# Gate matmuls whose f16 one-hot operands step by 4 bytes in place of 8

## The chip, the cores and the metric

The kernel runs on one core of a Trainium2 chip. What counts is the device time of one execution in microseconds (us); the number given is the median of three runs. The engines are TensorE (PE, with its weight loads PEld), VectorE (DVE), ScalarE (ACT), GpSimd (POOL) and SyncE (SP).

## What is computed

Two transformer blocks on 256 tokens of width 1,024. Each ends in a product-key retrieval ("peer"), which is where the change lies: for each token 8 heads pick 16 experts each out of 128 x 128, and the block adds a weighted sum over the picked experts.

```python
e = i1 * N_KEYS + i2                      # 8 heads x 16 picks per token
g = jax.nn.softmax(c_top, axis=-1)
ue = jnp.take(u, e, axis=0)
ve = jnp.take(v, e, axis=0)
act = gelu(einsum('thkd,td->thk', ue, xb))
return einsum('thk,thkd->td', g * act, ve)
```

## The kernel before

No row of `u` or `v` is gathered. The kernel multiplies all tokens with all experts, 128 experts of one `i2`-row at a time, and lets a gate be zero where a token did not pick an expert. The work of `Peer.run`, once in each of the two blocks:

- 16 tiles of the query projection, and on DVE the two rounds of top 16 (`retrieve`), whose result is, for each token, 128 pairs of indices (`self.ij`, f16) and 128 weights, held as two f16 numbers whose sum is the weight (`self.w`). The 128 picks of a token lie on the 128 partitions.
- 128 steps over `e`. Each is a tile of `u` times all tokens, `k.tile_ch()`: 24 matmuls (L187) of 256 columns, since every f32 operand is split into a high and a low part (`hi`, `lo`; `hi` is copied by ACT at L152, `lo` is subtracted by DVE at L157, two tiles ahead, three buffers each). Then `gelu` writes the activations into `a0` or `a1`. The tiles of `u` and `v` come by DMA, 512 KB each.
- 128 steps over the rows of `v`: 12 matmuls each (L261) of 512 columns.

The gates run in the background of the second part, by a generator (`gates`) that is advanced by a budget of DVE time after each tile (`k.step(BUD[0])`). For 8 tokens at a time DVE makes three f16 tiles of 1,024 elements in a partition: `o1`, the one-hot of the first index (L511), `ow[0]`, the one-hot of the second (L513), and twice its product with a weight part (L516, for `ow[1]` and then `ow[0]`). Per token two matmuls (L525) with `o1` as weights and `ow[0]`, `ow[1]` as moving operand add up the 128 x 128 gates of that token in PSUM; 4 tokens (`TB`) fill a bank, and 8 matmuls. DVE multiplies a bank into the activations that are there already (L531), ACT copies the gates of experts that are not yet computed (L533). The matmuls of a chunk are issued one chunk after its one-hots (`pend`). The tiles of one-hots have two buffers each.

A tile of one-hots lies as `[P, NB, P, TB]`: for each of `NB` = 2 groups of 4 tokens, 128 key values, and innermost the 4 tokens. The DVE instructions then run over 4 neighbouring elements, and a matmul, which wants the 128 key values of one token, reads every fourth element: a step of 4 f16, 8 bytes.

The order of instructions on each engine comes from a scheduler that simulates a timeline when the kernel is built; each engine runs its own list in order.

Of the kernel before, what the change touches and what calls it, by code (L numbers as in the profile page):

```python
# [11 lines left out]
F16 = mybir.dt.float16  # L12
# [7 lines left out]
P = 128  # L20
T = 256
# [386 lines left out]
BUD = [1.6, 1.6]  # L408
CUT = [0, 1024, 640]
TB = 4  # L410
NB = 2
LAST = 2
EARLY = 1
HB = 4
# [15 lines left out]
class Peer:  # L430
# [72 lines left out]
    def gates(self):  # L503

        k, nc = self.k, self.k.nc
        pend = deque()
        for t0 in range(0, T, NB * TB):
            o1, *ow = [self.oh.tile([P, NB, P, TB], F16, name=n, tag=n, bufs=2) for n in ("o1", "ow0", "ow1")]
            some = lambda a: a[:, t0:t0 + NB * TB].rearrange("p (b t) -> p b t", b=NB).unsqueeze(2).to_broadcast([P, NB, P, TB])
            iota = self.iota.unsqueeze(1).to_broadcast([P, NB, P, TB])  # L510
            nc.vector.tensor_tensor(out=o1, in0=iota, in1=some(self.ij[:, 0]), op=ALU.is_equal)  # L511
            yield 0.64
            nc.vector.tensor_tensor(out=ow[0], in0=iota, in1=some(self.ij[:, 1]), op=ALU.is_equal)  # L513
            yield 0.64
            for q in (1, 0):
                nc.vector.tensor_tensor(out=ow[q], in0=ow[0], in1=some(self.w[:, q]), op=ALU.mult)  # L516
                yield 0.64
            for n in range(NB):
                pend.append((t0 + n * TB, o1[:, n], [o[:, n] for o in ow]))
            while len(pend) > NB or (pend and t0 + NB * TB >= T):  # L520
                t1, o1, ow = pend.popleft()
                tag, g = k.bank([P, TB, P])
                for n in range(TB):
                    for q in range(2):
                        nc.tensor.matmul(out=g[:, n, :], lhsT=o1[:, :, n], rhs=ow[q][:, :, n], start=(q == 0), stop=(q == 1))  # L525
                yield 0.0
                ts = slice(t1, t1 + TB)
                gi = g.rearrange("p t i -> p i t")
                for a, lo, hi, e in self.slots(0, self.acted):
                    v = a[:, lo:hi, ts]  # L530
                    nc.vector.tensor_tensor(out=v, in0=gi[:, e:e + hi - lo], in1=v, op=ALU.mult)  # L531
                for a, lo, hi, e in self.slots(self.acted, P):
                    nc.scalar.activation(out=a[:, lo:hi, ts], in_=gi[:, e:e + hi - lo], func=ACTF.Copy)  # L533
                self.gated = t1 + TB
                k.done(tag)
                yield 0.00105 * TB * self.acted + 0.12
# [13 lines left out]
    def run(self, after):  # L550

        k, nc = self.k, self.k.nc
        b = self.b
        with ExitStack() as es:
            pool = lambda name: es.enter_context(k.tc.tile_pool(name=f"{name}{b}", bufs=1))
            self.oh = pool("oh")
            idx = pool("idx")
            self.iota = idx.tile([P, P, TB], F16, name="iota")
            self.k16 = k.const(idx, "iota16")
            self.ij = idx.tile([P, 2, T], F16, name="ij")  # L560
            self.w = idx.tile([P, 2, T], F16, name="w")
# [3 lines left out]
            tks = k.tc.tile_pool(name=f"tk{b}", bufs=1)  # L565
            tk = tks.__enter__()
            self.a0 = ap0.tile([P, SPLIT, T], F32, name="a0")
            nc.vector.tensor_copy(out=self.iota, in_=k.const(tk, "iota").unsqueeze(2).to_broadcast([P, P, TB]))
            skT = tk.tile([P, 16, P], F32, name="skT")
            nc.scalar.dma_start(out=skT, in_=k.i[f"sk{b}"])  # L570
            st = tk.tile([P, 2, 16, 16], F32, name="st")
# [67 lines left out]
            for n in range(P - LAST):  # L639
# [9 lines left out]
                a, w = parts.popleft(), k.weights()  # L649
# [984 lines left out]
```

## Time and profile before

| | |
|---|---|
| median of 3 runs (lowest, highest) | 2301.98 us (2300.34, 2302.52) |
| the profiled execution | 2302.45 us, of which the span of instructions is 2300.7 |
| granted TensorE clock, mean | 0.992 |
| busy, share of the span | PE 97%, PEld 90%, DVE 67%, ACT 51%, POOL 36% |
| moved by DMA | 370.90 MB, mean 161 GB/s |

Busy time of an engine is the union of its instructions' times. On PE matmuls overlap: a record lasts from a start to a modelled end, and the next one starts earlier than that. PEld are weight loads, which overlap with matmuls. Some few records can be missing from a trace. Durations are those of one profiled execution.

### The profile page before, as it was taken

The page shows a single profiled execution, that of the slowest core. Times are in us where ns is not written, and L with a number is a line of the kernel's source. Part 1 is how long each engine was busy: PE and PEld are TensorE (multiplying, and loading weights), DVE is VectorE, ACT ScalarE, POOL GpSimd, SP SyncE. Part 2 cuts the span into 40 slices and gives each one's busy share as a digit, 9 for nine tenths or more (in the row PEclk, how much of TensorE's full clock was granted, in tenths as well). Part 3 has the DMA queues.
Part 4 walks back from the last instruction along what each step waited for, and adds up shares of the span by engine and source line. Part 5 has one row for each costly group of instructions (what it writes and reads, how often), then busy time and mean ns, then how long its engine had stood idle before and what let it go on. Part 6 is the DMA issues. An engine that isn't in the chain of part 4 may idle for free. (4 is left out here: it accounts for less than half of the span.)

```text
span 2300.7 us, 41435 instructions
## 1 busy us (share of the span) xinstructions
PE 2234.7 (97%) x15512; PEld 2077.6 (90%) x15512; DVE 1543.4 (67%) x3119; ACT 1167.0 (51%) x2210; POOL 833.7 (36%) x626
## 2 busy tenths in 40 slices
PE   8999999999999999988899999999999999999998
PEld 8989999999988888878899898999999999888887
DVE  4669976788644544479756787699677885444444
ACT  5644544444455555565444555445444444555554
POOL 3453000000066666645553775620000000666665
PEclk9999999999999999999999999999999999999999
DMA  5455554444556666633334244556544445666664
GB/s 186 151 176 171 183 162 155 141 144 139 166 191 204 199 194 195 193 108 117 123 110 129 74 130 143 171 166 188 168 147 139 138 146 170 195 202 194 193 193 155
DMA packets 103881, 370.90 MB, mean 161 GB/s; under 512 B 12928, under 2 KB 14080, under 8 KB 103424
## 3 DMA queue, kind: packets, MB, share of 16 engines
q1 hardware_dynamic: 101808, 365.21, 50.6%
q10 hardware_dynamic: 1872, 3.04, 0.4%
q8 instruction: 122, 2.00, 0.3%
q14 instruction: 79, 0.65, 0.1%
HBM read 367.16 MB, written 1.05 MB: 160 GB/s over the span
## 5 line engine op out<-in xcount | busy, mean ns | idle before, releaser
L157 POOL TENSOR_TENSOR lo<-raw,hi 128x384 fp32r<-128x384 f32 (+2 forms) x428 | 706.9, 1654 | 1387.3 <-ACT hi L152 1348.2
L152 ACT ACTIVATE hi<-raw 128x1024 fp32r<-128x1024 f32 x684 | 724.3, 1060 | 741.9 <-PE mm L187 458.6
L187 PE MATMUL mm<-xh,hi 128*128 128x256 f32 x3168 | 919.6, 290 | 17.3 <-ACT cvx L1007 7.1
L187 PE MATMUL mm<-xh,lo 128*128 128x256 f32 x3168 | 902.5, 285 | 0.4 <-DVE lo L157 0.4
L187 PE MATMUL mm<-xl,hi 128*128 128x256 f32 x3168 | 897.4, 283 | 1.2 <-DVE xl L309 1.0
L157 DVE TENSOR_TENSOR lo<-raw,hi 128x640 fp32r<-128x640 f32 (+2 forms) x654 | 664.0, 1016 | 340.5 <-ACT hi L152 337.8
L187 PEld LDWEIGHTS mm<-xh,hi 128*128 128x128 f32 x3168 | 604.5, 191 | 22.2 <-ACT cvx L1007 8.7
L187 PEld LDWEIGHTS mm<-xl,hi 128*128 128x128 f32 x3168 | 605.4, 191 | 2.3 <-DVE xl L309 1.6
L187 PEld LDWEIGHTS mm<-xh,lo 128*128 128x128 f32 x3168 | 599.0, 189 | 0.6 <-DVE lo L157 0.6
L261 PE MATMUL y<-lo,ah 128*128 128x512 f32 x1024 | 398.4, 389 | 0.1
L261 PE MATMUL y<-hi,ah 128*128 128x512 f32 x1024 | 397.4, 389 | 0.0
L261 PE MATMUL y<-hi,al 128*128 128x512 f32 x1024 | 275.9, 389 | 0.0
L615 DVE TENSOR_TENSOR al<-a,ah 128x256 fp32r<-128x256 f32 x256 | 118.5, 464 | 191.4 <-PE y L261 191.0
L261 PEld LDWEIGHTS y<-lo,ah 128*128 128x128 f32 x1024 | 192.1, 188 | 40.7 <-POOL lo L157 0.6
L261 PEld LDWEIGHTS y<-hi,ah 128*128 128x128 f32 x1024 | 192.3, 188 | 39.9
L261 PEld LDWEIGHTS y<-hi,al 128*128 128x128 f32 x1024 | 192.2, 188 | 39.9
L614 ACT ACTIVATE ah<-a 128x256 fp32r<-128x256 f32 x256 | 106.5, 417 | 167.6 <-PE y L261 165.9
L525 PEld LDWEIGHTS <-o 128*128 128x128 f16 x1024 | 105.1, 118 | 6.9
L525 PE MATMUL by<-ow,o 128*128 128x128 f16 x672 | 94.8, 296 | 0.0
L516 DVE TENSOR_TENSOR ow<-ow,w 128x1024 f16<-128x1024 f16 x128 | 87.4, 685 | 0.1
L513 DVE TENSOR_TENSOR ow<-iota,ij 128x1024 f16<-128x1024 f16 x64 | 44.3, 692 | 54.5 <-PE by L525 38.6
L543 ACT ACTIVATE a<-mm 128x256 f32<-128x256 f32 (+33 forms) x228 | 69.0, 303 | 0.0
(500 smaller groups left out, 2006.7 us busy)
## 6 DMA issues: line engine op xcount, KB each, us to landing
raw<-in_u_dram SPq DMA_DIRECT2D x256, 512.0 KB, 3.5
raw<-in_v_dram SPq DMA_DIRECT2D x256, 512.0 KB, 4.3
raw<-in_w_in_dram SPq DMA_DIRECT2D x108, 512.0 KB, 3.5
raw<-in_wq_dram SPq DMA_DIRECT2D x32, 512.0 KB, 3.5
raw<-in_w_out_dram SPq DMA_DIRECT2D x16, 512.0 KB, 3.5
raw<-in_w_branch_a_dram SPq DMA_DIRECT2D x8, 512.0 KB, 3.5
raw<-in_w_branch_b_dram SPq DMA_DIRECT2D x8, 512.0 KB, 3.5
skT<-in_sk_dram ACTq DMA_DIRECT2D x2, 1024.0 KB, 5.2
```

The source lines that it names most:

```text
L152: self.nc.scalar.activation(out=h, in_=r, func=ACTF.Copy)
L157: eng.tensor_tensor(out=l[:, a:b], in0=r[:, a:b], in1=h[:, a:b].bitcast(F32), op=ALU.subtract)
L187: self.nc.tensor.matmul(out=ps, lhsT=a[:, c, :], rhs=b, start=(c == 0 and k == 0), stop=(c == NC - 1 and k == 2))
L261: i = self.nc.tensor.matmul(out=self.y[tt][dh], lhsT=p[:, ts], rhs=q[:, ds], start=(first and m == 0), stop=(last and m == 2))
L513: nc.vector.tensor_tensor(out=ow[0], in0=iota, in1=some(self.ij[:, 1]), op=ALU.is_equal)
L516: nc.vector.tensor_tensor(out=ow[q], in0=ow[0], in1=some(self.w[:, q]), op=ALU.mult)
L525: nc.tensor.matmul(out=g[:, n, :], lhsT=o1[:, :, n], rhs=ow[q][:, :, n], start=(q == 0), stop=(q == 1))
L543: nc.scalar.activation(out=a[:, s, n:T], in_=ps[:, n:T], func=ACTF.Gelu)
L614: nc.scalar.activation(out=h, in_=a, func=ACTF.Copy)
L615: nc.vector.tensor_tensor(out=l, in0=a, in1=h.bitcast(F32), op=ALU.subtract)
```

## The change

The tiles of one-hots lie with `OT` = 2 tokens innermost, `[P, 4, P, 2]` in place of `[P, 2, P, 4]`. A bank still holds 4 tokens, which now come from two groups. The operands of a gate matmul step by 2 f16, 4 bytes. The tiles keep their size, DVE's instructions their number and their 1,024 elements; `self.iota`, the table that the indices are compared with, has 256 elements in a partition in place of 512, and so has its copy. Built, the two kernels have the same instructions in the same order on every engine, but for that copy.

```diff
-NB = 2
+OT = 2
+NB = 8 // OT
...
-        for t0 in range(0, T, NB * TB):
-            o1, *ow = [self.oh.tile([P, NB, P, TB], F16, name=n, tag=n, bufs=2) for n in ("o1", "ow0", "ow1")]
-            some = lambda a: a[:, t0:t0 + NB * TB].rearrange("p (b t) -> p b t", b=NB).unsqueeze(2).to_broadcast([P, NB, P, TB])
-            iota = self.iota.unsqueeze(1).to_broadcast([P, NB, P, TB])
+        for t0 in range(0, T, NB * OT):
+            o1, *ow = [self.oh.tile([P, NB, P, OT], F16, name=n, tag=n, bufs=2) for n in ("o1", "ow0", "ow1")]
+            some = lambda a: a[:, t0:t0 + NB * OT].rearrange("p (b t) -> p b t", b=NB).unsqueeze(2).to_broadcast([P, NB, P, OT])
+            iota = self.iota.unsqueeze(1).to_broadcast([P, NB, P, OT])
...
-            for n in range(NB):
-                pend.append((t0 + n * TB, o1[:, n], [o[:, n] for o in ow]))
-            while len(pend) > NB or (pend and t0 + NB * TB >= T):
-                t1, o1, ow = pend.popleft()
+            one = lambda a, t: a[:, t // OT, :, t % OT]
+            for t1 in range(0, NB * OT, TB):
+                pend.append((t0 + t1, [[one(a, t1 + n) for a in (o1, *ow)] for n in range(TB)]))
+            while len(pend) > NB * OT // TB or (pend and t0 + NB * OT >= T):
+                t1, hot = pend.popleft()
...
-                        nc.tensor.matmul(out=g[:, n, :], lhsT=o1[:, :, n], rhs=ow[q][:, :, n], start=(q == 0), stop=(q == 1))
+                        nc.tensor.matmul(out=g[:, n, :], lhsT=hot[n][0], rhs=hot[n][1 + q], start=(q == 0), stop=(q == 1))
...
-            self.iota = idx.tile([P, P, TB], F16, name="iota")
+            self.iota = idx.tile([P, P, OT], F16, name="iota")
...
-            nc.vector.tensor_copy(out=self.iota, in_=k.const(tk, "iota").unsqueeze(2).to_broadcast([P, P, TB]))
+            nc.vector.tensor_copy(out=self.iota, in_=k.const(tk, "iota").unsqueeze(2).to_broadcast([P, P, OT]))
```

## Rows read from the trace of the kernel before

**Rows 1.** The page's head: busy us and share; granted clock in 40 slices.

```profile
PE 2234.7 (97%) x15512; PEld 2077.6 (90%) x15512; DVE 1543.4 (67%) x3119; ACT 1167.0 (51%) x2210; POOL 833.7 (36%) x626
...
PEclk9999999999999999999999999999999999999999
```

**Rows 2.** Instructions of L525: duration ns min/median/max, first and last start.

```profile
L525 PEld LDWEIGHTS <-o x1024: 111/117/141, 303.1 to 1904.6; 128*128 128x128 f16 x171
L525 PE MATMUL by<-ow,o x672: 277/297/304, 308.2 to 1904.7; 128*128 128x128 f16 x168
```

**Rows 3.** Stretches: length, busy PE, PEld, DVE, ACT, POOL, clock, DMA.

```profile
400.00:600.00 200.00, 200.00 (x1675) 197.54 (x1673) 157.82 (x294) 85.89 (x214) 0.00 (x0) 1.00 0.46 143
...
1800.00:1850.00 50.00, 50.00 (x421) 49.38 (x420) 40.95 (x76) 20.39 (x51) 0.00 (x0) 1.00 0.45 142
```

**Rows 4.** Waits: 400 to 600 us; those for L525, whole kernel; PE's own.

```profile
ACT hi L152 <- PE mm L187: 104.5, 54, 3.4
...
  DVE ow L513: 54.5, 58
...
PE mm L187 <- DVE lo L157: 0.4, 1, 0.4
```

**Rows 5.** Timeline of PE and PEld around gate matmuls: start us, length us.

```profile
507.30 2.05 PE L525 MATMUL bg<-ow,o 128*128 128x128 f16 x16
...
514.70 0.28 PE L187 MATMUL mm<-xl,hi 128*128 128x256 f32 x1
514.82 0.28 PE L187 MATMUL mm<-xh,lo 128*128 128x256 f32 x1
514.93 1.11 PE L525 MATMUL by<-ow,o 128*128 128x128 f16 x8
...
514.93 0.34 PEld L525 LDWEIGHTS <-o 128*128 128x128 f16 x4
...
515.75 0.21 PEld L187 LDWEIGHTS mm<-xh,hi 128*128 128x128 f32 x1
```

**Rows 6.** Timeline of PE in the second matmul stage.

```profile
900.54 0.39 PE L261 MATMUL y<-lo,ah 128*128 128x512 f32 x1
900.77 1.07 PE L261 MATMUL y<-hi,al 128*128 128x512 f32 x4
```

**Rows 7.** Loads of 64 f32 columns (timeline, durations); the page's row of L187 loads.

```profile
1269.37 0.54 PEld L1322 LDWEIGHTS bg<-hz 128*64 128x64 f32 x8
...
L1322 PEld LDWEIGHTS bg<-hz x8: 132/138/138, 1269.4 to 1269.8; 128*64 128x64 f32 x8
...
L187 PEld LDWEIGHTS mm<-xh,hi 128*128 128x128 f32 x3168 | 604.5, 191 | 22.2 <-ACT cvx L1007 8.7
```

**Rows 8.** Timeline of PE: matmuls of 64 columns at L1091, a pair and one.

```profile
1232.50 0.33 PE L1091 MATMUL by<-X,decc 128*128 128x64 f32 x2
...
1233.07 0.22 PE L1091 MATMUL by<-X,decc 128*128 128x64 f32 x1
```

**Rows 9.** One-hot instructions on DVE, 400 to 600 us: busy us, mean ns.

```profile
L516 DVE TENSOR_TENSOR ow<-ow,w 128x1024 f16<-128x1024 f16 x46 | 31.5, 685 | 0.0
...
L513 DVE TENSOR_TENSOR ow<-iota,ij 128x1024 f16<-128x1024 f16 x22 | 15.2, 693 | 18.3 <-PE by L525 13.3 <-PE bg L525 5.1
L511 DVE TENSOR_TENSOR o<-iota,ij 128x1024 f16<-128x1024 f16 x22 | 15.0, 682 | 0.0
```

**Rows 10.** Other 16-bit DVE instructions of 1,024 elements, 290 to 303 us.

```profile
L476 DVE TENSOR_TENSOR m<-abf,iota 128x1024 bf16<-128x1024 bf16 x2 | 2.4, 1222 | 0.0
L479 DVE TENSOR_TENSOR m<-m,itf 128x1024 bf16<-128x1024 bf16 x2 | 1.4, 690 | 0.0
```

**Rows 11.** Timeline of DVE over one chunk of the second stage; idle before in brackets.

```profile
1806.57 0.42 DVE L531 TENSOR_TENSOR a<-by,a 128x256 f32<-128x256 f32 x1 [1.11 <-PE by L525]
1807.40 0.69 DVE L513 TENSOR_TENSOR ow<-iota,ij 128x1024 f16<-128x1024 f16 x1 [0.41 <-PE by L525]
...
1814.20 0.42 DVE L531 TENSOR_TENSOR a<-by,a 128x256 f32<-128x256 f32 x1 [0.78 <-PE by L525]
```

## The prediction

> **What bounds the kernel now.** [...] Busy time of PE overstates, since matmuls are pipelined, so I went to the stage that the change touches. The gate matmuls (L525) are 1,024, 512 in each of the two Peer blocks, from 303 to 1,905 us [rows 2]. In the table of stretches, 400 to 600 us, the middle of the first gate stage, has PE busy 200.0 of 200.0 us at a granted clock of 1.00, VectorE (DVE) 157.8, ScalarE 85.9, GpSimd nothing; the busiest stretch of the second stage reads alike [rows 3]. The waits say the same from the other side: ScalarE stands 104.5 us in that stretch for PE to free a `hi` buffer, DVE's L513 alone 54.5 us in the whole kernel for gate matmuls, and PE waits once in the kernel, 0.4 us, for DVE's `lo` [rows 4]. In these stages everybody waits for PE's instruction stream, so what the stream loses in length, the kernel loses.
>
> So the question is the spacing of the gate matmuls, not their recorded duration. Sixteen of them take 2.05 us from the first start to the last end, eight 1.11 us; with 297 ns for the last one that is (2.05 - 0.297)/15 = 117 ns and (1.11 - 0.297)/7 = 116 ns each [rows 2, 5]. The expert matmuls beside them (L187, 256 columns) start 120 ns apart, those of L261 (512 columns) (1.07 - 0.39)/3 = 227 ns apart [rows 5, 6]. A gate matmul has 128 columns and costs as much as one of 256.
>
> **The change, part by part.**
>
> *The matmuls' moving operand.* [...] So I take 128 x 0.418 = 53.5 ns plus 10, 64 ns in place of 117.
>
> The bounds: nothing in the trace reads f16 at a step of 4 bytes. Lower end: eight pairs of load and matmul at L1322 start 57 ns apart, (0.54 - 0.138)/7 by their loads [rows 7], so loads and matmuls can follow that closely. Upper end: 117, no change. [...]
>
> [...]
>
> *The weight loads.* The gate's loads last 117 ns, those of f32 with 128 columns 191, those of f32 with 64 columns 138 [rows 2, 7]. With f32 loads of 64 columns a turn takes 57 ns, with one of 128 columns some 110 (below): the fixed part is some 80 ns and is overlapped. By the same deduction an f16 load occupies 117 - 80 = 37 ns. Inside a run it hides behind a stream of 53, at either step. Less step can only shorten it.
>
> At the end of a run it is different. The f32 load for the next L187 matmul starts together with the last gate matmul (515.75 us) [rows 5]. Such a load isn't done in 53 ns: at L1091 two matmuls of 64 columns, the second with an f32 load of 128 columns, take 0.33 us together where one takes 222 ns, 0.11 us between their ends [rows 8]. So the last gate matmul of a run goes from 117 to 110, not to 64: 46 ns of the saving are given back in each run. The timeline has the 1,024 in 130 runs (first and last as in [rows 2]).
>
> *The one-hots on DVE.* The same 256 instructions on 1,024 f16 elements, with 2 tokens innermost in place of 4. Now they take 682 to 693 ns; an f16-sized operation of the same count with 16 innermost takes 690, one whose innermost operand repeats a single value takes 1,222 [rows 9, 10]. Bounds: nothing, or 0.54 us each. A pair of tokens still steps by one element, as rows of 4 and of 16 do, and not by none: I take nothing.
>
> *DVE as the next bound.* In 400 to 600 us it has 157.8 us of work and PE loses 381 gate matmuls' saving, about 18 us, so it would be 157.8/182 = 87% busy; in the busiest 50 us 40.95/45.4 = 90% [rows 2, 3]. Its order of work shows where the room is: in the cycle from 1806.57 to 1814.20 us, 7.6 us long, it stands still twice, 0.78 and 0.40 us, both for the gate matmuls [rows 11], and the saving per cycle of 16 is 0.8 us at most. It fits, with some 0.3 us to spare; the `lo` tiles are prepared two tiles ahead, so a single late one costs nothing. I cost it at nothing; if the one-hots were dearer, that cover is gone (the rival below).
>
> *The rest.* `iota` is half as large, its copy half as long, twice in the kernel, outside PE's way. No instruction changes its place on any engine, no DMA is added.
>
> **The sum.** 1,024 x (117 - 64) = 54.3 us, less 130 x 46 ns = 6.0 us: 48.3 us. The profiled execution took 2302.45 us (span 2300.7), 0.5 above the median of 2301.98. 2302.45 - 48.3 = 2254.2, by the median 2253.7: I say 2254, faster by 2.1%.
>
> **The rivals.**
>
> *Nothing gained.* The 117 ns are not the stream but a chain of load and matmul: each load lasts as long as the spacing (117) and the next starts when a matmul starts [rows 2, 5]. Then the step changes nothing: 2302. Against it: four gate loads at the head of a run span 0.34 us, where a spacing of 117 would make it 0.47, so some of them lie much closer [rows 5], and f32 loads last 191 ns at a spacing of 120. [...]
>
> *Half of it.* The load of an f16 operand doesn't overlap a stream wholly: 53.5 + 37 = 90 ns a pair. 1,024 x 27 = 27.6, less 130 x 20 ns: 2277. For it: no row shows f16 pairs closer than 117. [...]
>
> *Slower: the one-hots double.* If an innermost pair takes DVE out of its fast way, 256 x 0.535 = 137 us are added on DVE. In 400 to 600 us that is 90 instructions [rows 9], 48 us on 158: 206 against PE's 182, DVE sets the pace, and PE waits for `lo` and for the next one-hots. Without a wait of its own left that stretch goes from 200 to 206, times 256/90 = 2.84 for both stages +17 us; with half of its present 42 us idle kept, +77 us. The middle is 2350. It decides from (182 - 158)/90 = 0.27 us per instruction, a one-hot of about 0.95 us. For it: 1,222 ns exists for such elements. Against it: it belongs to a step of nothing.
>
> **How the numbers follow.** The forecast 64%, half of it 14%, nothing 14%, slower 8%. A measurement of this kernel tells about 0.2%, 4.6 us, from no change. Faster by more is the first two: 0.78; within it 0.14; slower 0.08. The likeliest by itself lies between 2242 (58 ns, nothing given back at the runs' ends: 60.4 us off) and 2262. For 8 in 10 the range takes in half of it: 2240 to 2288; nothing gained and slower, 22%, stay out.
>
> **What would show it.** Right: eight gate matmuls in a row span about 0.7 us from the first start to the last end in place of 1.11, with a record near 230 ns each; PE stays at 50.00 of 50.00 in the stretches; one-hots at 682 to 693 ns; DVE near 90%, its waits for gate matmuls about half. The stretches outside the gates don't move. Wrong: spacing still 117 (the stream was not it); 80 to 90 (loads in the open); one-hots above 0.95 us, or new waits of PE for `lo` (DVE has become the bound).

## The result, and the profile after

The changed kernel takes 2249.98 us (four runs, 2247.33 to 2252.02) against 2302.25 before (now the median of four executions): a ratio of 0.9768, 95% interval 0.9756 to 0.9779, 52.3 us less. The forecast was 2254, 48.3 us less. Its profiled execution took 2248.88 us, with a span of 2247.1 where before it was 2300.7.

First the instructions of the gate matmuls, now L527, in the same view as [rows 2]: duration ns min/median/max, first and last start; the loads once for the whole kernel and once for each block.

```profile
L527 PEld LDWEIGHTS <-o x1024: 96/97/101, 302.3 to 1851.1; 128*128 128x128 f16 x171
L527 PE MATMUL by<-ow,o x672: 217/218/233, 306.6 to 1851.2; 128*128 128x128 f16 x168
...
L527 PEld LDWEIGHTS <-o x512: 96/97/101, 302.3 to 563.4; 128*128 128x128 f16 x171
...
L527 PEld LDWEIGHTS <-o x512: 96/97/101, 1590.0 to 1851.1; 128*128 128x128 f16 x171
```

A gate matmul's record fell from 297 to 218 ns, a load's from 117 to 97. The gate work of a block now runs for 261.1 us. Asked in the same way, the kernel before has these two rows, 288.1 and 288.0 us long:

```profile
L525 PEld LDWEIGHTS <-o x512: 112/117/141, 303.1 to 591.2; 128*128 128x128 f16 x171
...
L525 PEld LDWEIGHTS <-o x512: 111/117/139, 1616.6 to 1904.6; 128*128 128x128 f16 x171
```

27.0 and 26.9 us, together 53.9: the two gate stages hold the whole difference of the spans, 53.6 us. Outside them little moved: by the same rows the first gate load comes 0.8 us earlier, and from the last load of the first block to the first of the second it is 1,026.6 us where it was 1,025.4.

The timeline of PE in the kernel after, as in [rows 5], a run of eight, of one and of sixteen gate matmuls:

```profile
498.88 0.28 PE L187 MATMUL mm<-xh,lo 128*128 128x256 f32 x1
499.01 0.63 PE L527 MATMUL by<-ow,o 128*128 128x128 f16 x8
499.45 0.36 PE L187 MATMUL mm<-xh,hi 128*128 128x256 f32 x1
...
515.89 0.28 PE L187 MATMUL mm<-xh,lo 128*128 128x256 f32 x1
516.02 0.23 PE L527 MATMUL by<-ow,o 128*128 128x128 f16 x1
516.06 0.36 PE L187 MATMUL mm<-xh,hi 128*128 128x256 f32 x1
...
452.10 1.09 PE L527 MATMUL by<-ow,o 128*128 128x128 f16 x16
```

Eight take 0.63 us where they took 1.11, so a turn, the time from one start to the next, is (0.63 - 0.218)/7 = 59 ns, by sixteen (1.09 - 0.218)/15 = 58. The turn of 117 ns has halved.

Stretches of the kernel after, as in [rows 3], and its waits as in [rows 4] (the first two rows from 400 to 600 us, the next two for L527 in the whole kernel, the last PE's own):

```profile
400.00:600.00 200.00, 200.00 (x1840) 198.03 (x1839) 166.53 (x302) 95.19 (x223) 0.00 (x0) 1.00 0.54 163
...
500.00:550.00 50.00, 50.00 (x467) 49.36 (x466) 46.37 (x85) 22.92 (x59) 0.00 (x0) 1.00 0.53 158
...
1800.00:1850.00 50.00, 50.00 (x472) 49.36 (x472) 45.31 (x83) 23.20 (x59) 0.00 (x0) 1.00 0.51 159
```

```profile
ACT hi L152 <- PE mm L187: 95.9, 61, 2.5
DVE lo L157 <- ACT hi L152: 16.4, 16, 1.3
...
  DVE ow L514: 27.6, 28
  DVE a L533: 17.7, 40
...
PE mm L187 <- DVE lo L157: 0.4, 1, 0.4
```

PE is still busy without a gap and ScalarE still waits for it. (A gap shorter than the overlap of two records, some 0.16 us, would not show in such a row; the experiment with doubled matmuls below closes that.) DVE has come to 91% in the stretch from 1800 to 1850 us and to 93% in the busiest, 500 to 550 us; its L514 waits half as long for gate matmuls as L513 did, and PE waits for `lo` as little as before. The one-hots cost what they did (three of the rows from 400 to 600 us, as [rows 9]):

```profile
L517 DVE TENSOR_TENSOR ow<-ow,w 128x1024 f16<-128x1024 f16 x43 | 29.4, 685 | 0.0
L514 DVE TENSOR_TENSOR ow<-iota,ij 128x1024 f16<-128x1024 f16 x21 | 14.5, 693 | 7.3 <-PE by L527 5.2 <-PE bg L527 2.1
L512 DVE TENSOR_TENSOR o<-iota,ij 128x1024 f16<-128x1024 f16 x21 | 14.3, 682 | 0.0
```

### The profile page after: what moved, and what is told of

Same layout as the page of the kernel before. It is cut to its first block, busy times and chain, and to the rows that moved or that the text cites. A ratio compares the mean times of both kernels' runs of the same rounds, so it can differ in the third digit from the quotient of the medians.

```text
span 2247.1 us, 41435 instructions
## 1 busy us (share of the span) xinstructions
PE 2181.1 (97%) x15512; PEld 2025.8 (90%) x15512; DVE 1546.5 (69%) x3119; ACT 1166.4 (52%) x2210; POOL 829.3 (37%) x626
## 5 line engine op out<-in xcount | busy, mean ns | idle before, releaser
L187 PE MATMUL mm<-xh,hi 128*128 128x256 f32 x3168 | 918.8, 290 | 15.5 <-ACT cvx L1009 5.7
L187 PE MATMUL mm<-xh,lo 128*128 128x256 f32 x3168 | 902.8, 285 | 0.4 <-DVE lo L157 0.4
L187 PE MATMUL mm<-xl,hi 128*128 128x256 f32 x3168 | 898.8, 284 | 1.3 <-DVE xl L309 1.0
L187 PEld LDWEIGHTS mm<-xh,hi 128*128 128x128 f32 x3168 | 603.4, 190 | 19.6 <-ACT cvx L1009 6.8
L187 PEld LDWEIGHTS mm<-xl,hi 128*128 128x128 f32 x3168 | 604.0, 191 | 2.7 <-DVE xl L309 1.6
L187 PEld LDWEIGHTS mm<-xh,lo 128*128 128x128 f32 x3168 | 599.8, 189 | 0.6 <-DVE lo L157 0.6
L527 PEld LDWEIGHTS <-o 128*128 128x128 f16 x1024 | 59.6, 97 | 6.3
L514 DVE TENSOR_TENSOR ow<-iota,ij 128x1024 f16<-128x1024 f16 x64 | 44.3, 692 | 27.6 <-PE by L527 19.1
L533 DVE TENSOR_TENSOR a<-by,a 128x256 f32<-128x256 f32 (+15 forms) x144 | 47.8, 349 | 11.9 <-PE by L527 11.6
```

The source lines that it names most:

```text
L187: self.nc.tensor.matmul(out=ps, lhsT=a[:, c, :], rhs=b, start=(c == 0 and k == 0), stop=(c == NC - 1 and k == 2))
L527: nc.tensor.matmul(out=g[:, n, :], lhsT=hot[n][0], rhs=hot[n][1 + q], start=(q == 0), stop=(q == 1))
```

## The experiments

My theory: the stream of the moving operand sets the turn of a gate matmul, and its rate depends on the step in bytes. The rivals: the read of the weights does; a chain of load and matmul does; and, on the other engine, DVE has little room left.

**Each operand alone.** The tiles of the weights (`o1`) and of the moving operands (`ow0`, `ow1`) get a number of innermost tokens each.

```diff
-OT = 2
-NB = 8 // OT
+O1T, OWT = 4, 2        # e1: only the moving operands step by 4 bytes; e2: 2, 4
+GT = 8
...
+            o1, *ow = [self.oh.tile([P, GT // ot, P, ot], F16, name=n, tag=n, bufs=2) for n, ot in (("o1", O1T), ("ow0", OWT), ("ow1", OWT))]
```

> Only the moving operands ow0 and ow1 step by 4 bytes; the weights o1 step by 8 as before. If the moving operand's stream sets the spacing (my theory), the gate matmuls are 58 ns apart as in the changed kernel and the time is 2250 us (2247 to 2254). If the read of the weights sets it, spacing 117 ns and 2302 us. If both have to be short, something between, 75 to 117 ns, 2265 to 2302 us.

> The other half alone: the weights o1 step by 4 bytes, the moving operands by 8. Moving stream sets the spacing: 117 ns, 2302 us, as before the change. Weights set it: 58 ns and 2250 us. Both needed: between. By the way it tells which of the two shortened the records of the loads from 117 to 97 ns.

The moving operand alone: 2254.9 us (2253.88 to 2256.5), 0.9788 of the kernel before (0.9771 to 0.9804). The weights alone: 2303.76 us, 1.0002 (0.9992 to 1.0011). A run of sixteen in the timeline of PE, first of the kernel with short steps in the moving operand, then of the one with short steps in the weights:

```profile
493.90 1.15 PE L527 MATMUL bg<-ow,o 128*128 128x128 f16 x16
```

```profile
506.11 2.03 PE L527 MATMUL bg<-ow,o 128*128 128x128 f16 x16
```

The records of a matmul last 221 and 296 ns there, so the turns are (1.15 - 0.221)/15 = 62 ns and (2.03 - 0.296)/15 = 116. The moving operand's step carries the gain. The weights' step does next to nothing by itself, but once the stream is short it shows a little: 62 against 58 ns, by estimate 1,024 x 4 ns = 4 us, and the kernel lies 4.9 us above the changed one, a touch above the 2247 to 2254 that I had expected. Neither operand alone shortens the records of the loads to 97 ns: their median is 113 where only the moving operands step by 4 bytes, 115 where only the weights do. All gate operands are f16, so these runs don't tell a step in bytes from a step in elements; I go on in bytes.

**Further out: 16 bytes.** `OT = 8`, `NB = 1`; DVE reads the same table of 4 tokens twice for 8.

```diff
-OT = 2
+OT = 8
...
+            v = lambda a: a[:, 0].rearrange("p k (b t) -> p k b t", b=2)
+            nc.vector.tensor_tensor(out=v(o1), in0=iota, in1=some(self.ij[:, 0]), op=ALU.is_equal)
```

> All one-hots with 8 tokens innermost, a step of 16 bytes. [...] The one-hot instructions on VectorE stay at 682 to 693 ns.

2454.39 us, 1.0653 (1.0635 to 1.0671), slower than both times that I had estimated: 2302 us if 16 bytes cost no more than 8, and about 2410 if the stream, which I put at 2 x 53.5 = 107 of a turn's 117 ns, took twice as long. The instructions of L528 and a run of sixteen, then two stretches of the gate stages:

```profile
L528 PEld LDWEIGHTS <-o x1024: 141/146/176, 303.2 to 2055.1; 128*128 128x128 f16 x171
L528 PE MATMUL by<-ow,o x672: 392/413/451, 310.2 to 2055.3; 128*128 128x128 f16 x168
...
497.97 3.93 PE L528 MATMUL by<-ow,o 128*128 128x128 f16 x16
```

```profile
500.00:600.00 100.00, 100.00 (x655) 87.72 (x654) 63.46 (x117) 31.45 (x78) 0.00 (x0) 0.95 0.35 108
1900.00:2000.00 100.00, 100.00 (x639) 88.58 (x638) 62.10 (x115) 31.32 (x78) 0.00 (x0) 0.91 0.33 106
```

The turn is (3.93 - 0.413)/15 = 234 ns, twice that at 8 bytes. So 16 bytes do cost more than 8: from 4 to 16 bytes the turn goes with the step, 58, 117 and 234 ns. 1,024 x (234 - 117) = 120 us of the 151 are this. In the same stretches the granted clock stood at 0.95 and 0.91 on average, where the gate stages' stretches in the kernel before read 1.00 [rows 3], and the trace shows where it fell: for some of the expert matmuls that come shortly behind a run of gate matmuls. First the clock in such a place, then PE's timeline there:

```profile
490.85:493.50 2.65, 2.65 (x14) 2.65 (x13) 2.48 (x4) 0.00 (x0) 0.00 (x0) 0.50 0.00 0
...
491.22 0.42 PE L187 MATMUL mm<-xl,hi 128*128 128x256 f32 x1
491.44 0.42 PE L187 MATMUL mm<-xh,lo 128*128 128x256 f32 x1
...
493.77 0.28 PE L187 MATMUL mm<-xl,hi 128*128 128x256 f32 x1
493.89 0.28 PE L187 MATMUL mm<-xh,lo 128*128 128x256 f32 x1
```

At 0.50 they start 213 ns apart, from 493.77 us on 120, as in the kernel before. Leaving out the first behind each run, 290 L187 matmuls of the two gate stages start 205 to 220 ns before the next, and none in the kernel before: 290 x 93 ns = 27 of the other 31 us.

**The price of a turn, taken twice.** Every gate's two matmuls are made twice, the second pair over the first.

```diff
-                    for q in range(2):
+                    for q in (0, 1, 0, 1):
                         nc.tensor.matmul(out=g[:, n, :], lhsT=hot[n][0], rhs=hot[n][1 + q], start=(q == 0), stop=(q == 1))
```

> The changed kernel with every gate's two matmuls made twice, the second pair overwriting the first, so 2,048 gate matmuls and the same result. If PE's stream is the bound of the gate stages all through, each costs its spacing of 58 ns: 1,024 x 58 = 59 us more, 2309 us. If VectorE, 91% busy in the busiest stretch now, holds PE back in part of the stage, part of the 59 us is hidden: 2280 to 2300 us. By the 64 ns of my forecast it would be 2315 us.

2305.55 us, 1.0010 (1.0000 to 1.0019): 55.6 us above the changed kernel, 54 ns for each of the 1,024. A run of 32 takes 2.01 us, (2.01 - 0.218)/31 = 58 ns a turn:

```profile
443.63 2.01 PE L527 MATMUL by<-ow,o 128*128 128x128 f16 x32
```

That is some 4 us less than the 59 expected. The loads of each block, in the trace:

```profile
L527 PEld LDWEIGHTS <-o x1024: 96/97/101, 302.3 to 592.1; 128*128 128x128 f16 x171
...
L527 PEld LDWEIGHTS <-o x1024: 96/97/101, 1616.1 to 1906.0; 128*128 128x128 f16 x171
```

They run for 289.8 and 289.9 us in place of 261.1, together 57.5 more, 56 ns for each matmul. The rest of the difference lies outside the gate stages. So nearly the whole price is paid and next to nothing is hidden behind another engine: the stream is the bound of the gate stages all through the changed kernel.

**DVE's room.** One token innermost in all tiles (`OT = 1`), and in `o1` alone (`O1T, OWT = 1, 2`).

> One token innermost, so the key values of a token lie side by side and the gate operands step by 2 bytes; the scheduler, which costs these one-hots higher, places some gate matmuls otherwise (85 runs in place of 130). [...] For VectorE: each one-hot compares with a single repeated value and takes 1,222 ns in place of 685, 137 us more in all. By the rival of the forecast VectorE then sets the pace: 2310 to 2370 us. If VectorE had more room than I counted: 2250 us.

> Only o1, 64 of the 256 one-hot instructions, has one token innermost (1,222 ns expected); ow0 and ow1 stay at 4 bytes. VectorE gets 34 us more, in 400 to 600 us 22 x 0.54 = 12 us on 167. By the point of the forecast (room for 0.27 us on each of the four instructions of a chunk, here 0.13 on average) it is still hidden: 2250 us, at most 2255. If VectorE is the bound already in the busiest stretches, a part shows: 2260 to 2280 us.

All tiles: 2309.25 us, 1.0027 (1.0017 to 1.0038). Only `o1`: 2252.21 us, 0.9784 (0.9769 to 0.9799). From 400 to 600 us, the stretch and waits of the first kernel, then the same of the second:

```profile
400.00:600.00 200.00, 180.94 (x1650) 175.89 (x1649) 196.00 (x284) 84.90 (x199) 0.00 (x0) 0.99 0.46 140
...
PE mm L187 <- ACT ge L548: 18.1, 18, 1.7
ACT ge L548 <- DVE a L549: 13.1, 12, 2.2
```

```profile
400.00:600.00 200.00, 197.93 (x1815) 195.40 (x1815) 173.95 (x300) 92.62 (x218) 0.00 (x0) 1.00 0.53 159
...
PE mm L187 <- ACT ge L548: 2.1, 4, 0.7
```

In the first DVE is busy 196 of 200 us and PE is not: DVE sets the pace, one-hots there take 1,217 to 1,220 ns. PE's turn stays at (1.07 - 0.219)/15 = 57 ns:

```profile
438.52 1.07 PE L527 MATMUL by<-ow,o 128*128 128x128 f16 x16
```

So a step of 2 bytes gains 1 ns a turn over 4 bytes, nothing worth having. The time, 2309.25 us, falls just short of the 2310 to 2370 that I had expected. In the second kernel the 34 us more on DVE are nearly hidden, but PE waits 2.1 us in four places: the room that I counted is about what there is. And PE hardly waits for `lo` (0.7 us in the first kernel) and not for one-hots, as I had written, but for ScalarE's `gelu` (L548), which in the first kernel's rows waits for DVE's multiplication into the activations (L549) to free its `ge` buffer.

**Fewer runs of gate matmuls.** A bank's gate matmuls are ordered behind the expert matmuls issued so far, and the next tile's behind them: 78 runs in place of 130.

```diff
-                for n in range(TB):
+                with k.tc.issue_after(k.last_mm):
+                    for n in range(TB):
...
-                self.gelu(e, k.tile_ch())
+                with k.tc.issue_after(self.last_gate) if self.last_gate is not None else nullcontext():
+                    ps = k.tile_ch()
+                self.gelu(e, ps)
```

> The changed kernel with each bank's gate matmuls kept together between two expert tiles, which makes 78 runs of gate matmuls in place of 130. A run costs 49 ns more at its end than before the change, since the f32 load of the next expert matmul is no longer covered: 52 runs fewer give 52 x 49 ns = 2.5 us, 2247.5 us, if nothing waits for a gate that was put later or earlier. If the ends of runs cost nothing, no difference; if the fixed places make PE wait for a bank or a one-hot, slower than 2250 and PE idle in the trace.

2244.22 us, 0.9746 (0.9733 to 0.9759), a larger gain than the 2.5 us that I had expected. The changed kernel had not run side by side with it, so both ran again.

> The changed kernel as it is, measured again beside the one with 78 runs: 2250 us (2247 to 2253).

> The kernel with 78 runs of gate matmuls again, beside the changed kernel. In the traces a run of n gate matmuls costs 57 n + 69 ns over the expert matmul that follows, so 52 runs fewer are worth 52 x 69 ns = 3.6 us: 2246.4 us. The first measurement, 5.8 us below the changed kernel's, came from another session; if it holds, something besides the runs' ends is gained; if the two are within 2 us, the runs' ends are not worth what the trace says.

2249.45 us (0.9764, 0.9750 to 0.9777) and 2244.37 us (0.9744, 0.9730 to 0.9757): 5.1 us, where by the expectation the runs' ends give 3.6. One difference is in a stretch that neither kernel's gates touch. From 600 to 1590 us, first the changed kernel, then the one with 78 runs:

```profile
600.00:1590.00 990.00, 945.42 (x6249) 863.89 (x6248) 672.53 (x1416) 526.30 (x972) 522.31 (x428) 0.98 0.49 155
```

```profile
600.00:1590.00 990.00, 946.22 (x6273) 863.54 (x6272) 676.73 (x1418) 526.48 (x973) 520.71 (x428) 0.99 0.49 156
```

Its granted clock reads 0.98 and 0.99. The single executions point the same way. All five of the changed kernel had a mean granted clock of 0.990 or 0.991 and took 2249.52 us on average; the two of the other kernel at that clock took 2245.77, which is 3.7 us less, and its three at 0.993 took 2243.68. So at an equal clock about the 3.6 us of the runs' ends are left, as far as two executions can tell, and the higher clock comes with the rest; whether the edit raised it is open. The edit also moves the gates: their first load comes at 340.5 us, not at 303.5 as in the changed kernel. This kernel, at 0.9744 of the time before, is the fastest of the study, and side by side its slowest execution (2247.17 us) is faster than the changed kernel's fastest (2248.87).

## Why the prediction was right

*PE's stream is the bound.* Right: PE has no gap in the gate stages before or after, both stages shrank by the same 27 us, and doubled matmuls cost 56 ns each in the gate stages, nearly their whole turn.

*The moving operand's step sets the turn.* Right, and shown by the two operands taken apart: 62 ns with the moving operand alone, 116 with the weights alone. Twice the step made twice the turn, 58 ns at 4 bytes, 117 at 8 and 234 at 16; why, no run shows.

*The sum.* 48.3 us against 52.3 measured. The term that was mis-sized is the turn. My 53.5 ns for 128 columns was an estimate from the f32 matmuls of the kernel before, whose elements lie 4 bytes apart: by [rows 5, 6] 256 columns more take 227 - 120 = 107 ns, 0.418 each. That the gate's turn of 117 was near twice 53.5 at twice the step was the ground for it, and the 10 ns on top is what 117 has over 107. No run shows the 64 ns; measured are 57 to 59, some 4 above the 53.5; 57 is also the spacing of the L1322 pairs [rows 7], my lower bound. The term is 1,024 x (117 - 58) = 60.4 us, not 54.3. The other term, the ends of the runs, was too small in turn: in the timeline after, from the end of the L187 matmul ahead to the end of the one behind, one gate matmul makes 0.25 us and eight 0.65, so 57 ns each and 0.19 with none, where an L187 matmul alone takes 0.12. That is 0.07 us a run; before, eight made 1.06, by [rows 5] and the L187 matmul behind them, that is 0.12 with none:

```profile
515.79 0.37 PE L187 MATMUL mm<-xh,hi 128*128 128x256 f32 x1
```

With the turn of 57 that goes with it: 1,024 x 60 = 61.4, less 130 x 0.07 = 9.1, is 52.3 us. So two misses partly cancelled, 7.1 us too little for the turn and 3.1 too little for the ends, and the total was nearer than its terms.

*One-hots for nothing, DVE with room.* Right in both: 682 to 693 ns as before, and 91 to 93% in place of the 90% forecast. The price of one token innermost, 1,220 ns, was the one read from [rows 10]. With it in all tiles the kernel took 2309 us, the matmuls' gain included, where I gave that rival 2350 and 17 us over the kernel before at the least; measured are some 6. That its wait would be for `lo` and one-hots was wrong: it is for `gelu`.

*Nothing gained.* This rival rested on a chain of load and matmul. The runs exclude it: with the weights unchanged and loads of 113 ns a turn fell to 62.

*Half of it.* Loads in the open would have made 90 ns a turn; measured are 57 to 59 over runs of up to 32, so they are covered.

## What to carry to other kernels

When a matmul of few columns costs as much as one with twice as many (here 117 ns against 120), look at the step of its moving operand early (here, for f16, a turn took 58 ns at 4 bytes and 117 at 8), and compare spacings of starts, not durations of records. Lay the tile out for the matmul as far as the engine that writes it stays in its fast way: two f16 innermost gave both here, four cost PE twice the turn, one cost DVE 1.8 times the instruction (1,220 ns against 685). Where PE is the bound, look also at how many runs the short matmuls make: here each run cost some 0.07 us at its end, by my reading for the load of the next large matmul (191 ns), which the short ones no longer cover, and 78 runs in place of 130 took 5.1 us less, of which the ends explain 3.6.

## What the runs showed of the hardware

- The turn of a 128-column f16 matmul was 57 ns at a step of 2 bytes (where the weights stepped by 2 as well), 58 at 4, 117 at 8 and 234 at 16. A step of 16 bytes was as much worse than 8 as 8 than 4, which I had not expected. Whether bytes or elements count was not tried.
- With the 16-byte step PE's granted clock averaged 0.95 and 0.91 in stretches in which PE had no gap, and fell to 0.50 shortly behind runs of matmuls of 234 ns a turn; the expert matmuls that followed started 213 ns apart in place of 120. At 8 and 4 bytes the stretches from 400 to 600 us, which PE fills, read 1.00.
- The step of the weights showed only under a short stream: 62 ns against 58 a turn, with loads of 113 against 97 ns; under the long one it was 117 against 116, with loads of 117 against 115.
